# Where a norm's factor is applied in a hybrid Mamba/attention layer: on the gates by their activation, on dt, x, B and C by the eviction

## The chip, the cores and the metric

The kernel runs on one core of one Trainium2 chip. Its time is the device time of one execution in microseconds (us); the span is the part of it that the profiler's records cover. PE is the tensor engine, PEld its weight loads, DVE the vector engine, ACT the scalar engine, POOL the GpSimd engine, SP the engine that issues most of the loads.

## The reference

One layer over 512 tokens with 2048 channels, all in float32. Only the head of it matters here:

```python
h = rmsnorm(x, norm_w)          # x * rsqrt(mean(x*x) + EPS) * norm_w, one factor for each token
u = h @ w_in
z_ssm, xbc, dt_f, dt_b, q_a, kv_a, z_attn, g_ssm, g_attn = split(u)
xbc = silu(dwconv(xbc, conv_w, conv_b))      # depthwise over tokens, 4 taps
dt  = softplus(dt + dt_bias)                 # both directions
...                                          # bidirectional SSD on x, B, C, dt; silu(z_ssm) gates it
...                                          # latent attention on q_a, kv_a; silu(z_attn) gates it
y   = (ssd @ w_ps) * sigmoid(g_ssm) + (attn @ w_pa) * sigmoid(g_attn)
out = rmsnorm(x + y @ w_out)
```

The norm multiplies each token by one factor R = rsqrt(mean(x*x) + EPS). A product with h is the product with x * norm_w, with each token's result multiplied by R.

## The kernel before

Float32 products are made of three matmuls of a rounded type: each operand is split into a high part (ACT, `h` or `wh`) and a low part (DVE or POOL, `l` or `wl`), and `mm3` (L168 to L170) adds high*high, high*low and low*high in one PSUM bank. One product here means 16 such steps over the 2048 channels, 48 matmuls of 128x512, for 128 output columns and all 512 tokens. Its weights come as two chunks of 128x1024 (`wchunk`, L158 to L165): a load on SP's queue, a cast on ACT, a subtraction on DVE (on POOL while `ahead[0]` is 0, at the very start). There are three buffers of each.

The program in the order of time:

- **Head.** `cst` and `vec` come on ACT's queue. x is loaded row by row (tokens on partitions) in eight pieces (L208). For each of four token tiles ACT squares and sums the two halves (L210), DVE and ACT make the factor (L212 to L213, `small_rsqrt` L183 to L192), and L220 (DVE) or L218 (ACT) multiplies x by it in place. PE then turns x over by 64 transposes (L225) through all eight PSUM banks; ACT writes h's high part with norm_w multiplied in (L229), DVE its low part (L230), both out of PSUM.
- **First products.** First the product for dt (`dtp`), then six products of group 0 (x tiles, B and C: `xbc_gen`), each followed by the four taps of the convolution (`conv_silu`, L388 to L392: ACT with a bias, three DVE steps, ACT's Silu) and a store. Beside these products `h_sums` (L710 to L730) builds h = h_h + h_l again and from it the operand sums S1, S2, S3 and S4, and `dt_make` (L282 to L300) makes the softplus of dt in some 18 DVE steps.
- **Gates.** Three gate weights `wz`, `wgs` and `wga` of 2048x2048. Each takes two column pairs, and each pair is a Strassen-Winograd scheme of seven products (P1, P5, P6, P2, P3, P7, P4) with operands x11, x12, x22 (quadrants of h), S1, S2, S4 (held) and S3, which is loaded back from DRAM into the place of quadrant x21 at the start of `wz`; x21 is loaded and split again at the end of `wga` (`h_back`). Each result of 128x512 (tokens on partitions) passes `gate`, an activation (Silu or Sigmoid) and a store.
- **The rest.** Four groups of SSD with the other products as filling, attention, two projections, the merge, the output projection and the last norm.

The order of PE's instructions is the order of the code. A scheduler places the instructions of the other engines by priority; `tc.high_priority(offset=AHEAD)` puts the weights' chunks ahead, and `keep_in_program_order` fixes single instructions. Pools of SBUF buffers set when a buffer comes free.

## Time and profile before

| what | value |
|---|---|
| time, median of 3 runs | 2065.09 us (2063.13 to 2066.34) |
| the profiled execution's own time | 2063.24 us |
| its span | 2061.4 us |
| PE busy | 1968.5 us, 95% of the span |
| DVE busy | 1461.8 us, 71% |
| ACT busy | 967.9 us, 47% |
| POOL busy | 317.4 us, 15% |
| first matmul of a product (`dtp`) | 32.82 us after the span's start |

The page cuts the span into 40 slices of 51.5 us, with the busy share of each engine in tenths. A timeline row gives start, duration, engine, line, operation, output and inputs, shape and count, and in brackets the idle time before it with what ended it. A group row gives count, busy time and the mean ns of one. A row of windows gives, for a stretch of time, the busy time of PE, PEld, DVE, ACT and POOL with their counts, then the granted clock of PE, the share of the DMA engines and GB/s.

### The profile page before, as it was taken

The page shows a single profiled execution, that of the slowest core. Times are in us where ns is not written, and L with a number is a line of the kernel's source. Part 1 is how long each engine was busy: PE and PEld are TensorE (multiplying, and loading weights), DVE is VectorE, ACT ScalarE, POOL GpSimd, SP SyncE. Part 2 cuts the span into 40 slices and gives each one's busy share as a digit, 9 for nine tenths or more (in the row PEclk, how much of TensorE's full clock was granted, in tenths as well). Part 3 has the DMA queues.
Part 4 walks back from the last instruction along what each step waited for, and adds up shares of the span by engine and source line. Part 5 has one row for each costly group of instructions (what it writes and reads, how often), then busy time and mean ns, then how long its engine had stood idle before and what let it go on. Part 6 is the DMA issues. An engine that isn't in the chain of part 4 may idle for free.

```text
span 2061.4 us, 24706 instructions
## 1 busy us (share of the span) xinstructions
PE 1968.5 (95%) x9074; PEld 1627.2 (79%) x9074; DVE 1461.8 (71%) x1946; ACT 967.9 (47%) x1351; POOL 317.4 (15%) x337
## 2 busy tenths in 40 slices
PE   6999999999989999998999999999999999999998
PEld 5888888888868787786788878888877777888886
DVE  7976676676669789698687567666676888776342
ACT  6444444444445656445546344444444454443232
POOL 0001010010043152241331101110010201100120
PEclk9999999999999999998999999999999999999999
DMA  5568657656547847686464857783376876865332
GB/s 195 165 179 200 175 124 192 192 116 182 140 162 189 250 124 205 207 226 201 154 183 153 236 156 200 206 219 90 86 210 249 301 248 264 273 217 169 107 118 82
DMA packets 166585, 378.56 MB, mean 184 GB/s; under 512 B 16001, under 2 KB 65281, under 8 KB 165889
## 3 DMA queue, kind: packets, MB, share of 16 engines
q1 hardware_dynamic: 104688, 238.33, 35.4%
q0 software_dynamic: 26944, 92.29, 20.5%
q10 hardware_dynamic: 34832, 46.38, 6.2%
q8 instruction: 71, 1.16, 0.2%
q14 instruction: 50, 0.40, 0.1%
HBM read 325.03 MB, written 98.04 MB: 205 GB/s over the span
## 4 chain that ended last, share of the span: by engine, by line
PE 71%; DVE 13%; DMA 9%; issue 4%; ACT 3%; SPq 1%; POOL 0%; ACTq 0%; DVEq 0%; POOLq 0%
PE P L564 10%; PE P L565 10%; PE P L563 10%; PE f L1492 3%; PE f L1493 3%; PE f L1491 3%; PE za L168 2%; PE za L169 2%; DVE sum L999 2%; PE za L170 2%; PE xbc L168 2%; PE xbc L169 2%; PE xbc L170 2%; DVE wl L164 2%; DMA wraw<-wps 1%
## 5 line engine op out<-in xcount | busy, mean ns | idle before, releaser
L434 DVE TENSOR_TENSOR wl<-X,wh 128x1024 fp32r<-128x1024 f32 x152 | 185.3, 1223 | 84.5 <-ACT wh L433 83.9
L433 ACT CAST wh<-X 128x1024 fp32r<-128x1024 f32 x152 | 159.5, 1053 | 157.7 <-PE P L565 137.7
L164 DVE TENSOR_TENSOR wl<-wraw,wh 128x1024 fp32r<-128x1024 f32 (+2 forms) x148 | 172.7, 1167 | 85.7 <-ACT wh L163 85.3
L163 ACT CAST wh<-wraw 128x1024 fp32r<-128x1024 f32 (+2 forms) x150 | 145.1, 969 | 138.9 <-PE za L169 41.2
L434 DVE TENSOR_TENSOR wl<-wraw,wh 128x1024 fp32r<-128x1024 f32 x74 | 91.5, 1236 | 96.4 <-ACT wh L433 96.2
L168 PE MATMUL xbc<-h_h,wh 128*128 128x512 f32 x384 | 152.6, 397 | 0.0
L170 PE MATMUL xbc<-h_h,wl 128*128 128x512 f32 x384 | 150.5, 392 | 0.0
L169 PE MATMUL xbc<-h_l,wh 128*128 128x512 f32 x384 | 150.3, 391 | 0.0
L434 DVE TENSOR_TENSOR wl<-Y,wh 128x1024 fp32r<-128x1024 f32 x80 | 97.9, 1224 | 72.9 <-ACT wh L433 72.8
L564 PE MATMUL P<-wl,h_h 128*128 128x512 f32 x384 | 149.5, 389 | 0.0
L565 PE MATMUL P<-wh,h_l 128*128 128x512 f32 x384 | 149.5, 389 | 0.0
L563 PE MATMUL P<-wh,h_h 128*128 128x512 f32 x384 | 149.5, 389 | 0.0
L433 ACT CAST wh<-wraw 128x1024 fp32r<-128x1024 f32 x74 | 77.9, 1053 | 144.4 <-PE f L1493 69.3
L433 ACT CAST wh<-Y 128x1024 fp32r<-128x1024 f32 x80 | 84.2, 1054 | 111.7 <-PE P L565 96.8
L564 PE MATMUL P<-wl,S 128*128 128x512 f32 x288 | 112.4, 390 | 0.6 <-DVE wl L434 0.6
L565 PE MATMUL P<-wh,S 128*128 128x512 f32 x288 | 112.1, 389 | 0.0
L563 PE MATMUL P<-wh,S 128*128 128x512 f32 x288 | 112.1, 389 | 0.0
L168 PE MATMUL za<-h_h,wh 128*128 128x512 f32 x256 | 102.0, 398 | 0.0
L170 PE MATMUL za<-h_h,wl 128*128 128x512 f32 x256 | 100.5, 392 | 0.1
L169 PE MATMUL za<-h_l,wh 128*128 128x512 f32 x256 | 100.2, 391 | 0.0
L999 DVE TENSOR_TENSOR_SCAN sum<-da,scn 128x512 f32<-128x512 f32 x64 | 86.7, 1368 | 0.0
L170 PEld LDWEIGHTS xbc<-h_h,wl 128*128 128x128 f32 x384 | 72.6, 189 | 15.5
(634 smaller groups left out, 5187.8 us busy)
## 6 DMA issues: line engine op xcount, KB each, us to landing
wraw<-wi SPq DMA_DIRECT2D x102, 512.0 KB, 4.1
da<-da_d SPq DMA_DIRECT2D x64, 256.0 KB, 4.6
T_wps<-wps POOLq DMA_DIRECT2D x32, 512.0 KB, 6.2
T_wpa<-wpa POOLq DMA_DIRECT2D x32, 512.0 KB, 9.4
wraw<-wo SPq DMA_DIRECT2D x32, 512.0 KB, 3.5
wraw<-wps SPq DMA_DIRECT2D x24, 512.0 KB, 5.2
xbc_d<-xbc ACTq DMA_DIRECT2D x24, 256.0 KB, 3.5
wraw<-wun SPq DMA_DIRECT2D x16, 384.0 KB, 3.1
```

What stands on the lines that cost most here:

```text
L163: act.copy(h, raw)
L164: (dve if ahead[0] else pool).tensor_sub(l, raw, h.bitcast(F32))
L168: pe.matmul(out, wh, xh, start=start, stop=False)
L169: pe.matmul(out, wh, xl, start=False, stop=False)
L170: pe.matmul(out, wl, xh, start=False, stop=stop)
L433: act.copy(hi_, raw)
L434: dve.tensor_sub(lo_, raw, hi_.bitcast(F32))
L563: pe.matmul(bs[i], xh, wh, start=(j == 0), stop=False)
L564: pe.matmul(bs[i], xh, wl, start=False, stop=False)
L565: pe.matmul(bs[i], xl, wh, start=False, stop=(j == 7))
L999: dve.tensor_tensor_scan(sums[dd], flat(da), mask, 0.0, ALU.add, ALU.mult)
L1491: pe.matmul(acc, mh, wh, start=(start and k == 0), stop=False)
```

## The change

The host gives x a second time, transposed (`xt`: eight pieces of 128 channels x 2 x 512 tokens). The kernel loads these in place of x, interleaved with the chunks of the first three products' weights. There are no transposes any more. h_h and h_l now hold x * norm_w without the factor R, and are made from SBUF as each piece lands (L236 on ACT, L237 on DVE). ACT squares each piece (L240), POOL adds up the eight squares (`sq_sum`, L242, seven additions of 128x1024), eight small matmuls sum them over the partitions (`square_sums`, L251), and four matmuls with a diagonal spread the factor over the partitions (`factor`, L264), which ACT copies to R and stores (`r_d`). The first three products (tiles 4, 5 and 0 of group 0) go side by side in three banks in a fixed order of their steps; tiles 1, 2, 3 and then dt follow one after the other.

The factor is applied in four places: `xbc_done` multiplies the bank by R on DVE (L752) ahead of the convolution, where before the convolution read the bank itself; `dt_make` multiplies dt by R, and moves from the first products to the second pair of `wz`, with its input and R loaded back from DRAM; `gate` gives the activation R as its scale (`r4`, one number for each token on a partition); and at the last pair of `wga` hooks load all four quadrants of x * norm_w from DRAM, multiply them by R (x11 and x12 on POOL, x21 and x22 on DVE, L828) and split them anew into h_h and h_l, so that the products behind the gates find h there as before. For this x_t is multiplied by norm_w in place (16 DVE steps, L765) and stored as four quadrants (8 stores on ACT's queue, L214). `h_sums` takes its sums from x_t and has no additions of h_h and h_l any more.

Matmuls of 128x512 ahead of the gates are the same in number (eight products) but for 3 short warming ones, 8 of square_sums and 4 of factor; 64 transposes are gone.

The diff, cut to its core:

```diff
-    xs_t = []
-    for t in range(TT):
...
-    tps = [mm(), mm(), mm(), pa(), pa(), pb(), pb(), pc()]
...
+    def sxq(name):
+        n_q[0] ^= 1
+        return sx.tile([P, 1024], F32, tag=f"q{n_q[0]}", bufs=1, name=name)
+    n_q = [1]
+    def put(dst, t):
+        act.dma_start(dst, t)
+    R, v_x, sq_sum = (sx.tile([P, n], F32, name=nm) for n, nm in ((SEQ, "R"), (SEQ, "v_x"), (1024, "sq_sum")))
+    warm_ps = pc("warm")
+    dve.memset(v_x, 1.0)
+    for _ in range(3):
+        pe.matmul(warm_ps, v_x[:, 0:P], v_x, start=True, stop=True)
+    ahead[0] = 1
+    firsts_i = (T_XBC + 4, T_XBC + 5, T_XBC)
+    early = [[] for _ in firsts_i]
+    for j in range(8):
+        for n, at in ((0, 0), (1, 2), (2, 4), (0, 4), (1, 6)):
+            if at == j:
+                early[n].append(wchunk(a["wi"][firsts_i[n], len(early[n])], 1024))
+        xs = x_t[:, 2 * j:2 * j + 2, :].rearrange("p k t -> p (k t)")
+        nc.sync.dma_start(xs, a["xt"][j])
+        for k in (2 * j, 2 * j + 1):
+            nw = vec[:, V_NORM + k:V_NORM + k + 1]
+            act.activation(h_h[:, k, :], x_t[:, k, :], AF.Copy, scale=nw)
+            dve.scalar_tensor_tensor(h_l[:, k, :], x_t[:, k, :], nw, h_h[:, k, :].bitcast(F32), ALU.mult, ALU.subtract)
+        for i in ([j - 1] if 0 < j < 7 else [6, 7] if j else []):
+            sq = sxq("sq") if i else sq_sum
+            act.activation(sq, x_t[:, 2 * i:2 * i + 2, :].rearrange("p k t -> p (k t)"), AF.Square)
+            if i:
+                pool.tensor_add(sq_sum, sq_sum, sq)
+    early[2].append(wchunk(a["wi"][firsts_i[2], 1], 1024))
+    r4 = few(4)
...
+    def square_sums():
+        ss = pa("ss")
+        for t in range(TT):
+            for k in range(2):
+                pe.matmul(ss[:, t:t + 1], sq_sum[:, k * SEQ + t * P:k * SEQ + (t + 1) * P], ones[:, 0:1],
+                          start=(k == 0), stop=(k == 1))
+        v4, rt = few(4), few(4)
+        dve.tensor_scalar(v4, ss[:, 0:4], 1.0 / D, EPS, ALU.mult, ALU.add)
+        new = {"rt": rt, "rr": r4}
+        small_rsqrt(v4, 4, lambda n: new[n])
+        for t in range(TT):
+            dve.tensor_scalar_mul(v_x[:, t * P:(t + 1) * P], ident, r4[:, t:t + 1])
+    def factor():
+        rp = pc("rp")
+        for t in range(TT):
+            pe.matmul(rp[:, t * P:(t + 1) * P], ones, v_x[:, t * P:(t + 1) * P], start=True, stop=True)
+        act.copy(R, rp)
+        put(r_d, R)
...
+    dt_t = []
+    def dt_make():
+        v, e = st("dv_"), st("e")[0:64, :]
+        u, pl = (sum_tile("p1") for _ in range(2))
+        nc.sync.dma_start(v, dv_d)
+        nc.sync.dma_start(u, r_d)
+        dve.tensor_mul(v, v, u)
+        put(kr_d, v[64:128, :])
+        v, u, pl = (t[0:64, :] for t in (v, u, pl))
+        da64 = u
+        act.activation(v, v, AF.Identity, bias=vec[0:64, V_DTB:V_DTB + 1])
...
-        def whole(name, i, j):
-            t = sxq(name)
-            h, l = part_of(i, j, q)
-            dve.tensor_add(view4(t), h.bitcast(F32), l.bitcast(F32))
-            return t
         ks = slice(4 * q, 4 * q + 4)
         cs = slice(q * 1024, (q + 1) * 1024)
+        def x(i, j):
+            return x_t[:, 8 * j + 4 * q:8 * j + 4 * q + 4, i * 256:(i + 1) * 256]
         def keep(w, t):
             split_into(s_op[w][:, 0, ks], s_op[w][:, 1, ks], view4(t))
...
+        s1, s3 = sxq("s1"), sxq("s3")
+        tc.keep_in_program_order(dve.tensor_sub(view4(s1), x(1, 0), x(1, 1)))
+        keep("S1", s1)
+        tc.keep_in_program_order(dve.tensor_sub(view4(s3), x(0, 0), x(1, 0)))
         put(h_d["S3"][:, cs], s3)
-        dve.tensor_sub(x11, x22, x11)
-        keep("S2", x11)
-        x12 = whole("x12", 0, 1)
-        dve.tensor_add(x12, x12, x11)
-        keep("S4", x12)
-    for i in range(5):
-        run(xbc_gen(0, (4, 5, 0, 1, 2, 3)[i], sxt))
-        if i in (1, 3):
-            h_sums(i // 2)
-    dt_make(sxd)
+        s2 = sq_sum
+        dve.tensor_sub(view4(s2), view4(s1), x(0, 0))
+        keep("S2", s2)
+        dve.tensor_add(view4(s1), view4(s2), x(0, 1))
+        keep("S4", s1)
...
+    def xbc_done(i, p_):
+        dve.tensor_mul(v_x, p_, R)
+        o = st("xbc")
+        put(xbc_d[0][i], conv_silu(v_x, (0, 1, 2, 3, 16, 20)[i], o, lambda n: o))
+    firsts = [mm("xbc") for _ in range(3)]
+    order = "AAAABBBB" + "AABB" * 2 + "C" * 8 + "A" * 8 + "B" * 8 + "C" * 8
+    for i in together([gemm_steps(p_, win(t), h_h, h_l, w_) for p_, t, w_ in zip(firsts, firsts_i, early)], order):
+        if i == 31:
+            square_sums()
+        if i == 42:
+            factor()
+    ahead[0] = AHEAD
+    for k in range(KT):
+        tc.keep_in_program_order(dve.tensor_scalar_mul(x_t[:, k, :], x_t[:, k, :], vec[:, V_NORM + k:V_NORM + k + 1]))
+    for q in range(2):
+        for n, (j, i) in (("x11", (0, 0)), ("x12", (1, 0)), ("x21", (0, 1)), ("x22", (1, 1))):
+            put(view4(h_d[n][:, q * 1024:(q + 1) * 1024]), x_t[:, 8 * j + 4 * q:8 * j + 4 * q + 4, i * 256:(i + 1) * 256])
+    for i, p_ in zip((4, 5, 0), firsts):
+        xbc_done(i, p_)
+    for i in (1, 2, 3):
+        p_ = mm("xbc")
+        if i < 3:
+            h_sums(i - 1)
+        run(gemm_steps(p_, win(T_XBC + i), h_h, h_l))
+        xbc_done(i, p_)
+    dtp = mm("dtp")
...
+            act.activation(o, o, f, scale=r4[:, t:t + 1])
             put(dst[t][b], o)
         return done
...
+    r_back = []
+    def r_load():
+        r_back.append(st("R"))
+        nc.sync.dma_start(r_back[0], r_d)
+    def h_load(which, tag="w", in_order=False):
+        def f():
+            h_ops.raws[which] = []
+            for q in range(2):
+                t = w_tile(tag)
+                made = nc.sync.dma_start(t, h_d[which][:, q * 1024:(q + 1) * 1024])
+                if in_order:
+                    tc.keep_in_program_order(made)
+                h_ops.raws[which].append(t)
+        return f
+    def h_scale(which, i, eng):
+        def f():
+            for t in h_ops.raws[which]:
+                eng.tensor_mul(view4(t), view4(t), r_back[0][:, i * 256:(i + 1) * 256].unsqueeze(1).broadcast_to([P, 4, 256]))
+        return f
+    def h_new(which, i, j):
+        return lambda: [h_part(which, i, j, q) for q in range(2)]
...
+    gates[0].hooks = {(0, "P5"): [h_load("S3", in_order=True), h_new("S3", 1, 0)], (1, "P5"): [dt_make]}
+    gates[2].hooks = {(1, "P1"): [r_load, h_load("x11"), h_scale("x11", 0, pool), h_new("x11", 0, 0)],
+                      (1, "P2"): [h_load("x12"), h_scale("x12", 0, pool), h_new("x12", 0, 1)],
+                      (1, "P3"): [h_load("x21"), h_scale("x21", 1, dve)],
+                      (1, "P7"): [h_new("x21", 1, 0), h_load("x22", "Y"), h_scale("x22", 1, dve)],
+                      (1, "P4"): [h_new("x22", 1, 1)]}
     gates[0].first_columns(0)
-    run(xbc_gen(0, 3, None))
-    for p_ in gates:
+    first_pair = gates[0].pair(0)
+    for _ in range(24):
+        next(first_pair)
+    dv_ = st("dv_")
+    act.copy(dv_, dtp)
+    put(dv_d, dv_)
+    run(first_pair)
+    run(gates[0].pair(1))
...
```

Three places show how instructions now stand on an engine.

**Head, DVE.** Before, x was scaled (L220) and the sixteen low parts of h (L230) came out of PSUM banks in one row, the last ones of it interleaved with two chunks of weights:

```order
L220 TENSOR_SCALAR xt3_290<-xt3_290,small_65 128x1024
L230 SCALAR_TENSOR_TENSOR h_l_233<-mm_307,vec_226,h_h_232 128x512
L230 SCALAR_TENSOR_TENSOR h_l_233<-mm_308,vec_226,h_h_232 128x512
L230 SCALAR_TENSOR_TENSOR h_l_233<-mm_309,vec_226,h_h_232 128x512
L230 SCALAR_TENSOR_TENSOR h_l_233<-pa_310,vec_226,h_h_232 128x512
L230 SCALAR_TENSOR_TENSOR h_l_233<-pa_311,vec_226,h_h_232 128x512
```

Now, from the first instruction on (`wl` are low parts of weights, `h_l` those of h, x4 counts repeats):

```order
L221 MEMSET v_x 128x512
L891 TENSOR_SCALAR small<-vec 128x8
L164 TENSOR_TENSOR wl<-wraw,wh 128x1024
L237 SCALAR_TENSOR_TENSOR h_l<-x_t,vec,h_h 128x512 x4
L164 TENSOR_TENSOR wl<-wraw,wh 128x1024
L237 SCALAR_TENSOR_TENSOR h_l<-x_t,vec,h_h 128x512 x4
L164 TENSOR_TENSOR wl<-wraw,wh 128x1024
L237 SCALAR_TENSOR_TENSOR h_l<-x_t,vec,h_h 128x512 x2
L164 TENSOR_TENSOR wl<-wraw,wh 128x1024
L237 SCALAR_TENSOR_TENSOR h_l<-x_t,vec,h_h 128x512 x2
L164 TENSOR_TENSOR wl<-wraw,wh 128x1024
L237 SCALAR_TENSOR_TENSOR h_l<-x_t,vec,h_h 128x512 x4
```

On POOL seven additions (L242) stand where two subtractions of weights (L164) stood. The low parts are made from x_t in SBUF, with the weights between them, and POOL has seven additions beside them. The next row on DVE is the last early chunk, then the chain of the factor.

**The stores of x_t, ACT.** Around the end of the third product, now, with the semaphores that are waited for in brackets (DMAHW is a transfer):

```order
L214 DMA h_x12_199<-x_t_248 128x4x256 [waits DVE_49]
L265 COPY R_252<-rp_514 128x512 [waits PE_49]
L214 DMA h_x22_201<-x_t_248 128x4x256
L214 DMA r_d_361<-R_252 128x512 [waits Activation_49]
L214 DMA h_x11_198<-x_t_248 128x4x256 [waits DMAHW1_49]
L214 DMA h_x12_199<-x_t_248 128x4x256 [waits DMAHW2_49,DVE_49]
L163 CAST wh_630<-wraw_628 128x1024
L214 DMA h_x21_200<-x_t_248 128x4x256 [waits DMAHW3_49]
L214 DMA h_x22_201<-x_t_248 128x4x256 [waits DMAHW5_49]
L397 ACTIVATE xbc_561<-v_x_253,vec_228 128x512 [waits DVE_49]
L163 CAST wh_682<-wraw_680 128x1024 [waits PE_49]
L163 CAST wh_712<-wraw_710 128x1024 [waits PE_49]
```

None of these stores was there; the row before had `h_x21` and `h_S3` stores one at a time between casts. Casts of weights (L163) and the first step of the convolution (L397) are queued behind them.

**Last pair of wga, DVE, from P2's sums to P3's chunks.** Before:

```order
L591 TENSOR_TENSOR p5_3894<-p5_3894,u_3964 128x512
L591 TENSOR_TENSOR p5_3896<-p5_3896,u_3965 128x512
L434 TENSOR_TENSOR wl_4032<-wraw_4029,wh_4031 128x1024
L434 TENSOR_TENSOR wl_4057<-Y_3818,wh_4056 128x1024
L434 TENSOR_TENSOR wl_4074<-Y_3837,wh_4073 128x1024
L619 TENSOR_TENSOR p1_3812<-p1_3812,P2_3970 128x512
L619 TENSOR_TENSOR p1_3814<-p1_3814,P2_3971 128x512
L434 TENSOR_TENSOR wl_4091<-Y_3856,wh_4090 128x1024
```

Now:

```order
L603 TENSOR_TENSOR p5_3837<-p5_3837,u_3907 128x512
L603 TENSOR_TENSOR p5_3839<-p5_3839,u_3908 128x512
L442 TENSOR_TENSOR wl_3975<-wraw_3972,wh_3974 128x1024
L442 TENSOR_TENSOR h_l_235<-wraw_3997,h_h_234 128x4x256
L442 TENSOR_TENSOR wl_4010<-Y_3761,wh_4009 128x1024
L828 TENSOR_TENSOR wraw_4085<-wraw_4085,R_3747 128x1024
L442 TENSOR_TENSOR wl_4027<-Y_3780,wh_4026 128x1024
L634 TENSOR_TENSOR p1_3743<-p1_3743,P2_3913 128x512
L634 TENSOR_TENSOR p1_3745<-p1_3745,P2_3914 128x512
L442 TENSOR_TENSOR h_l_235<-wraw_3999,h_h_234 128x4x256
L442 TENSOR_TENSOR wl_4044<-Y_3799,wh_4043 128x1024
L828 TENSOR_TENSOR wraw_4087<-wraw_4087,R_3747 128x1024
```

Between the chunks of P2 and P3 (`wl` from `wraw` and from `Y`) there are now two splits of x11 (L442 with `h_l`) and two multiplications of x21 by R (L828); the loads, the multiplications on POOL and the casts on ACT ahead of the splits are other engines' rows.

151 lines of the change are left out of this document (51 added, 100 removed).

## Prediction

> **What bounds the kernel now.** The page's engine shares come first, then the waits of PE in the first 66 us, then the timeline of that stretch.
>
> ```profile
> PE 1968.5 (95%) x9074; PEld 1627.2 (79%) x9074; DVE 1461.8 (71%) x1946; ACT 967.9 (47%) x1351; POOL 317.4 (15%) x337
> PE   6999999999989999998999999999999999999998
> ...
> PE mm L225 <- DVE xt L220: 19.4, 4, 11.0
> ```
>
> PE is busy for 95% of the span, so what moves the end is a hole in PE's work. The largest stands in the first slice (6): PE waits 19.4 us there, in four pieces, for DVE's scaled x. Everything behind waits for that, since PE's order is fixed.
>
> ```profile
> 7.77 0.17 DVE L824 TENSOR_SCALAR small<-vec 128x8 f32<-128x8 f32 x1 [7.77 <-DMA vec<-vec]
> 11.04 0.90 PE L225 MATMUL mm<-cst,xt 128*128 128x128 f32 x3 [11.04 <-DVE xt L220]
> 18.33 1.03 ACT L163 CAST wh<-wraw 128x1024 fp32r<-128x1024 f32 x1
> 19.43 4.64 POOL L164 TENSOR_TENSOR wl<-wraw,wh 128x1024 fp32r<-128x1024 f32 x2 [18.55 <-ACT wh L163]
> 19.68 2.11 DVE L188 TENSOR_TENSOR small<-small 128x1 f32<-128x1 f32 x1
> 21.83 2.26 DVE L189 TENSOR_TENSOR small<-small 128x1 f32<-128x1 f32 x1
> 24.12 0.15 DVE L190 TENSOR_SCALAR small<-small 128x1 f32<-128x1 f32 x1
> 25.32 0.91 PE L225 MATMUL mm<-cst,xt 128*128 128x128 f32 x3 [6.31 <-DVE xt L220]
> 25.83 1.84 ACT L229 ACTIVATE h_h<-mm,vec 128x512 fp32r<-128x512 f32 x3
> 31.83 2.06 DVE L230 SCALAR_TENSOR_TENSOR h_l<-mm,vec,h_h 128x512 fp32r<-128x512 f32 x3
> 32.82 0.47 PE L168 MATMUL dtp<-h_h,wh 128*128 128x512 f32 x1
> 36.44 1.22 DVE L164 TENSOR_TENSOR wl<-wraw,wh 128x1024 fp32r<-128x1024 f32 x1
> 43.83 0.39 PE L168 MATMUL xbc<-h_h,wh 128*128 128x512 f32 x1
> ```
>
> From 32.82 on PE runs without a hole: one product takes 43.83 - 32.82 = 11.0 us, so a step of three matmuls takes 0.69 us. Note 19.68: two DVE operations on 128x1, which take 0.16 us elsewhere, end only as POOL's two subtractions do, one POOL subtraction each (4.64 / 2 = 2.32 us).
>
> ```profile
> 585.73 2.04 POOL L932 TENSOR_TENSOR xw<-xT,wst 128x512 f32<-128x512 f32 x2 [5.76 <-ACT xT L887]
> 587.73 5.93 POOL L965 TENSOR_TENSOR yo<-xT,dsk 128x512 f32<-128x512 f32 x4
> 589.69 2.06 DVE L164 TENSOR_TENSOR wl<-wraw,wh 128x1024 fp32r<-128x1024 f32 x1
> 598.19 1.21 DVE L164 TENSOR_TENSOR wl<-wraw,wh 128x1024 fp32r<-128x1024 f32 x1
> 663.88 3.27 POOL L1008 TENSOR_TENSOR G<-dtT,cbb 128x512 f32<-128x512 f32 x2 [11.95 <-DVE cbb L987]
> 664.78 1.53 DVE L999 TENSOR_TENSOR_SCAN sum<-da,scn 128x512 f32<-128x512 f32 x1
> 667.81 1.21 DVE L999 TENSOR_TENSOR_SCAN sum<-da,scn 128x512 f32<-128x512 f32 x1
> ```
>
> It shows again later: the same subtraction takes 1.21 us alone and 2.06 beside POOL. So a DVE operation with two inputs in SBUF and a POOL operation take turns here, each whole.
>
> **The change, part by part. The new head.** The measure is the end of the third product: 32.82 + 3 x 11.0 = 65.8 us before. Behind it both kernels still have five products, then the gates, in PE's work.
>
> Loads don't set it. Before, 4.2 MB of x and the first chunks came at about 420 GB/s:
>
> ```profile
> GB/s 0 163 289 372 407 339 423 412 418 421 426 418 76 0 0 199 188 311 0 0 0 0 0 11 0 30 298 350 257 126 0 96 191 371 128 259 90 259 90 109
> ```
>
> Each number covers 1.5 us. Now eight pieces and six chunks, 7.3 MB, take some 18 us at that rate and are there by about 21 us.
>
> ACT makes 16 h_h at 0.62 us (1.84 / 3), 5 casts at 1.0 and 8 squares at the 1.0 of a cast of that size, one or two squares behind the last h_h: from 7.8 us (vec gives norm_w) the last h_h is ready near 30 us.
>
> DVE makes 16 h_l at 0.69 us (2.06 / 3), 11.0 us, and 5 weight subtractions at 1.14 (1.22 less the overlap of neighbours), 5.7 us. POOL makes 7 additions at 2.32, 16.2 us. Before, h_l read one input from PSUM; now both tensors lie in SBUF, and none of the rows is of this operation beside POOL. Bounds: if h_l takes turns with POOL, the sum is 11.0 + 5.7 + 16.2 = 33 us from about 8, so 41 us; if POOL's addition costs the 2.04 / 2 = 1.02 us for 512 that L932 shows, 39 us; if h_l doesn't take turns, ACT sets it and the last addition ends near 33 us. I take 41, as the subtractions of two SBUF inputs are the nearest rows.
>
> The Trainium skill, page SBUF — State Buffer, section Who interferes with whom, says of this that DVE's second port is GpSimd's and that the lock is exclusive; the trace agrees with it at 19.68 and 589.69 us (2.06 for 1.21). By that rule the additions and h_l exclude each other; no run here shows it for this operation yet, and without the rule the forecast would rest on the subtractions alone.
>
> From the last h_l PE has one step left of the first product's second half, 8 small matmuls and 4 of 128 columns x 512 for the factor (0.4 and 0.9 us by the 128x128 rows: 0.90 / 3 each, overlapped), and 16 steps x 0.69 = 11.0: 41 + 0.7 + 0.4 + 0.9 + 11.0 = 54.0 us. **Gain at the head: 65.8 - 54.0 = 11.8 us**, 13.7 with the cheaper POOL, 20 without turns (last addition at 33, and 12.4 behind it: 45.7).
>
> **From the fourth product to the gates.** Before, DVE is full there:
>
> ```profile
> 60.00:80.00 20.00, 20.00 (x90) 16.58 (x89) 20.00 (x20) 14.15 (x16) 0.00 (x0) 1.00 0.44 150
> ...
> L710 DVE TENSOR_TENSOR x<-h_h,h_l 128x1024 f32<-128x1024 f32 x8 | 9.6, 1218 | 0.0
> L391 DVE SCALAR_TENSOR_TENSOR cacc<-xbc,vec,cacc 128x511 f32<-128x511 f32 x23 | 17.0, 738 | 0.1
> L220 DVE TENSOR_SCALAR xt<-xt,small 128x1024 f32<-128x1024 f32 x6 | 4.3, 752 | 0.1
> L292 DVE SCALAR_TENSOR_TENSOR pl<-pl,u 64x512 f32<-64x512 f32 x8 | 5.4, 679 | 0.1
> ```
>
> PE has 20.00 of 20 us, though, as this work began in the first product. Removed: 8 additions of L710 (9.6 us) and the 18 or so steps of dt_make at 0.68 (12 us). Added: 16 scalings by norm_w at about 0.42 (half of 752 ns and a fixed part), 6.7 us; 6 multiplications by R at 0.68, 4 us. Nothing of the operand sums can begin ahead of the scalings. These and the chain of the factor (7 small operations, about 3.5 us) lie beside the 11.8 us that PE needs from square_sums to the fourth product, almost to the end. Behind it: 14 steps of h_sums and 7 weight subtractions, 21 x 1.14 = 24 us, and 24 operations of 512 at 0.66, 16 us: 40 us of DVE in the four remaining products' 43.7 us, before DVE can split the gates' first four chunks. It doesn't wait only for itself: ACT's casts stand behind its stores, and each tap chain goes ACT, DVE three times, ACT. If its gaps add up to 9 us, PE waits about 4 to 5 us; if there are none, 0; a fully serial ACT and DVE would cost 9. **I take a loss of 3.5 us**, nearer to the filled row above, which had no hole on PE.
>
> **Gates.** The scale of the 48 activations lies on ACT, which has room:
>
> ```profile
> 480.00:500.00 20.00, 20.00 (x90) 16.58 (x89) 13.01 (x15) 9.89 (x12) 3.46 (x4) 1.00 0.86 214
> 500.00:520.00 20.00, 20.00 (x90) 16.56 (x89) 16.47 (x15) 10.17 (x12) 0.00 (x0) 1.00 0.16 30
> 520.00:540.00 20.00, 20.00 (x90) 16.55 (x89) 14.07 (x15) 8.44 (x9) 2.59 (x3) 1.00 0.64 167
> 540.00:560.00 20.00, 20.00 (x90) 16.58 (x89) 13.39 (x15) 11.84 (x14) 0.86 (x1) 1.00 0.56 150
> sum 80.00, PE 80.00 PEld 66.27 DVE 56.93 ACT 40.34 POOL 6.91; mean PE 20.00 PEld 16.57 DVE 14.23 ACT 10.08 POOL 1.73
> L187 DVE RECIPROCAL rr<-rt 128x512 f32<-128x512 f32 x2 | 6.7, 3352 | 2.1 <-ACT rt L185 2.0
> ```
>
> In the last pair, 480 to 560 us, DVE is idle for 80 - 56.9 = 23 us, ACT for 40. Added there on DVE: 6 splits and 4 multiplications at 1.22, 12.2 us; on POOL 4 multiplications of 2.32, 9.3 us, which shut DVE out by turns. Together 21.5 of the 23 us, so mean load allows it. But the first split of x11 stands on DVE between P2's and P3's chunks and waits there for SP's load and POOL's multiplication; P3's chunks are queued behind it, and PE waits for these. Bounds: 0, and 9.3 if all of POOL's time lands on PE; I take 1.7. In wz's second pair dt_make brings 18 steps of 0.68 and a reciprocal of 3.35, 15 us, into gaps of about 5.8 of 20 us: 0 to 2, I take 0.5. The 12 extra DMAs of 512 KB on SP and ACT (4 MB in, 4 MB out) meet a DMA share of 0.16 to 0.86; they cost nothing unless the landing that the split above waits for comes late, which is in its bounds. Behind the gates all order is as before.
>
> **Sum:** 11.8 - 3.5 - 1.7 - 0.5 = 6.1 us less than the profiled 2063.24, 2057.1. Its median of runs stands 1.85 above that execution, so **2059 us**.
>
> **The rivals.** (A) *h_l doesn't take turns with POOL.* For it: SCAN at 664.78, with both inputs in SBUF, takes 1.53 beside POOL and not 3; it isn't a plain tensor operation either. Against it: 1.53 isn't 1.21. Head gain 20 in place of 11.8: 2059 - 8.2 = 2051 us.
>
> (B) *DVE becomes the bound from the fourth product to the gates' end and takes the gain back.* For it: DVE's 20.00 of 20 us above, and sums that start 20 us later than before. Against it: 10 us less DVE work in all. Loss at its bounds, 9 + 2 instead of 3.5 + 2.2, gives 2059 + 5.3 = 2064 us.
>
> (C) *ACT's queue is held by the stores.* The eight stores of x_t and that of R stand in order on ACT's queue, and four of them wait for an earlier transfer to land before ACT may go on to casts. What landings cost:
>
> ```profile
> h_x<-x ACTq DMA_DIRECT2D x2, 512.0 KB, 3.1
> h_S<-s ACTq DMA_DIRECT2D x1, 512.0 KB, 5.6
> ```
>
> One chunk of the fourth product is cast ahead of them, 5.5 us of cover. Four waits of 3.1 hold ACT for 12.4 us and PE for 6.9; four of 5.6 for 22.4 and 16.9. It then stands in place of the 3.5: 11.8 - 16.9 - 2.2 = 7.3 us of loss, 2072 us. It decides from a landing of (11.8 - 2.2 + 5.5) / 4 = 3.8 us each. Against it: the stores of the first half can start while DVE scales the second, so some waits are over by then.
>
> **How the numbers follow.** Runs of this kernel differ by 3.2 us, so 0.2% (4.1 us: below 2061.0 or above 2069.2) is what can be told from no change. Forecast 0.50, of which 0.42 falls below 2061.0 and 0.08 above; A 0.15, all faster; B 0.20, 0.17 the same and 0.03 slower; C 0.15, 0.10 slower and 0.05 the same. Faster 0.57, same 0.30, slower 0.13. The range reaches from 2048 (A with the cheaper addition) to 2067 (B and half of C).
>
> **What would show it.** PE's first product starts near 10 us, and its step 33 near 42 (forecast) or 34 (A). An h_l beside a POOL addition lasts 2 us or more, or 0.75. The fourth product starts near 54. Waits of PE for L164 or L442 between 54 and 105 add up to 3 or 4 us; with C the casts L163 stand behind L214, with stores that land later than 3.8 us. In the last pair of wga the only new wait is P3's first chunk. Wrong would be a hole at a place that has none here: in PE between 20 and 40 us for a load, or behind the gates.

## Result: slower by 1.1%, and the profile after

| | median of runs | profiled execution | span |
|---|---|---|---|
| before | 2065.72 us (2063.13 to 2067.85, 4 runs) | 2063.24 us | 2061.4 us |
| changed | 2092.19 us (2081.42 to 2094.03, 4 runs) | 2091.57 us | 2089.7 us |

The ratio is 1.0113, with a 95% interval of 1.0084 to 1.0141. The medians alone give 1.0128. The forecast was 2059 us, with a range from 2048 to 2067. The page after, its first rows:

```profile
PE 1982.2 (95%) x9040; PEld 1627.2 (78%) x9040; DVE 1490.4 (71%) x1950; ACT 975.8 (47%) x1345; POOL 342.6 (16%) x346
...
PE   8999989999989999998999989999989999999998
```

The hole at the start is smaller (8 where it was 6), and a new one stands in the sixth slice (261 to 313 us, the place of dt_make; two more in the 24th and the 30th, where both kernels have the same instructions). PE's waits over the whole span:

```profile
PE P L575 <- DVE wl L442: 18.0, 16, 3.8
PE P L574 <- ACT wh L442: 16.3, 5, 4.3
...
PE xbc L169 <- DVE h_l L237: 6.7, 5, 1.8
PE dtp L170 <- DVE wl L164: 4.5, 1, 4.5
```

Before, the first two (then L564 and L563) were 5.4 and 6.7 us, and the dt product never waited. Ahead of the gates stand seven products, six of group 0 and dt (one sentence on the change counts eight, and the prediction once five behind the third where there are four; its sum used four). PE's order behind them is the same in both kernels, so the start of the same matmul can be compared in the two traces. The lag of the changed kernel, after less before:

| place on PE | lag, us | change of the lag |
|---|---|---|
| fourth product starts (57.7, was 65.6) | -7.9 | -7.9 |
| P1 of wz starts (111.5, was 109.1) | +2.4 | +10.3 |
| P5 of wz | +4.9 | +2.5 |
| from wz's second pair into wgs's first | +21.2 | +16.3 |
| just ahead of wga's second pair | +21.4 | +0.2 |
| end of its P7 | +29.7 | +8.3 |
| behind the holes that follow the gates in both (614.9, was 587.8) | +27.0 | -2.7 |
| end | +28.2 | +1.2 |

Two words for what follows. A hole is the time from the start of one matmul on PE to the start of the next, less the usual 0.23 us; the waits above give some 0.2 us less for the same hole. Half clock is a stretch in which the trace grants PE half of its clock; in the head a matmul then starts every 0.43 us, not every 0.23.

**Head.** The timeline of the changed kernel, DVE, POOL and PE:

```profile
30.10 9.09 DVE L237 SCALAR_TENSOR_TENSOR h_l<-x_t,vec,h_h 128x512 fp32r<-128x512 f32 x4
39.11 1.21 DVE L164 TENSOR_TENSOR wl<-wraw,wh 128x1024 fp32r<-128x1024 f32 x1
...
29.06 8.92 POOL L242 TENSOR_TENSOR sq_sum<-sq_sum,sq 128x1024 f32<-128x1024 f32 x3 [0.56 <-ACT sq L240]
...
35.81 0.50 PE L169 MATMUL xbc<-h_l,wh 128*128 128x512 f32 x1 [1.80 <-DVE h_l L237]
...
38.58 0.80 PE L169 MATMUL xbc<-h_l,wh 128*128 128x512 f32 x1 [1.80 <-DVE h_l L237]
...
40.88 3.41 PE L251 MATMUL ss<-cst,sq_sum 128*128 128x1 f32 x16
```

Four h_l take 9.1 us beside three additions of POOL, 2.3 us each where one takes 0.7 alone: they take turns, and the last ends at 39.1 us. PE waits for the low parts twice for 1.8 us, and then its matmuls take 0.63 us, not 0.39. The windows show why (PEclk is the third number from the end):

```profile
37.00:48.00 11.00, 9.42 (x31) 8.17 (x32) 6.82 (x16) 1.25 (x2) 0.97 (x1) 0.53 0.26 79
48.00:54.00 6.00, 6.00 (x31) 5.02 (x30) 5.76 (x15) 0.00 (x0) 0.00 (x0) 1.00 0.72 260
54.00:79.00 25.00, 25.00 (x114) 20.75 (x113) 13.56 (x16) 10.52 (x12) 0.00 (x0) 1.00 0.67 229
79.00:103.00 24.00, 19.53 (x82) 15.82 (x81) 23.96 (x26) 10.95 (x12) 0.00 (x0) 0.91 0.24 89
96.00:101.00 5.00, 0.53 (x3) 0.13 (x1) 5.00 (x6) 1.04 (x1) 0.00 (x0) 0.78 0.37 123
101.00:106.00 5.00, 5.00 (x13) 3.91 (x14) 3.63 (x5) 1.44 (x2) 0.00 (x0) 0.53 0.82 272
```

PE's granted clock is about half behind the holes: in 37 to 48 us, and again in 101 to 106 us, just after the dt product waited 4.5 us for DVE. DVE has gaps from 54 to 79 us (13.6 of 25 busy) and none from 79 to 103 (23.96 of 24). In the whole span the trace has 91.7 us of half clock, before 65.9; the last 6.4 and 7.9 us of these lie behind PE's last matmul and cost nothing, the others cost about half their length while PE has work. The place tells more than the total. From 31.5 us, where the records of the clock begin in the trace before, to the end of the gates, the changed kernel does 31.0 us of PE's work at half clock, the one before none. Behind the gates it is 36.4 us, before 44.0.

**Ahead of P1, ACT:**

```profile
108.41 0.59 ACT L847 COPY dv__1021<-dtp 128x512 f32<-128x512 f32 x1 [3.01 <-PE dtp L170]
...
109.39 0.63 ACT L401 ACTIVATE xbc<-xbc 128x512 f32<-128x512 f32 x1 [0.40 <-ACT dv__1021 L847]
...
110.42 2.94 ACT L442 CAST wh<-X 128x1024 fp32r<-128x1024 f32 x3 [0.40 <-ACT xbc L401]
```

The casts of P1's first weights stand behind the copy of the dt product, which waits for that product's end, and behind the last convolution's Silu. PE stands still from the end of the dt product, 108.4 us, to 111.5 us: a hole of 3.3 us. Another of 1.0 us and 3.4 us of half clock follow behind P1's first matmul.

**dt_make, in wz's second pair:** first SP's wait, then DVE.

```profile
SPq L284 <- DMA zs_d<-p: 11.2, 1, 11.2
...
249.94 0.69 DVE L285 TENSOR_TENSOR dv__1618<-dv__1618,p 128x512 f32<-128x512 f32 x1 [6.95 <-DMA p<-r_d]
...
255.33 3.35 DVE L295 RECIPROCAL p<-p 64x512 f32<-64x512 f32 x1
...
280.99 0.69 DVE L608 TENSOR_TENSOR p<-p,P 128x512 f32<-128x512 f32 x1 [3.94 <-DMA da_d<-p]
```

Its two buffers are p1 buffers, of which there are two. The load of R (L284) waits 11.2 us on SP until a gate's result has been stored out of one; DVE then waits 7.0 us for that load, with weights behind it. Later P3's sum (L608) waits 3.9 us for the store of dt_make's own result. PE has holes of 3.0, 0.8, 1.2, 1.2, 4.5 and 1.0 us there, and half clock at 252 and 293 us.

**Last pair of wga.** Ahead of P3, POOL and DVE:

```profile
549.20 2.87 POOL L828 TENSOR_TENSOR wraw<-wraw,R 128x1024 f32<-128x1024 f32 x1 [30.09 <-DMA wraw<-h_x]
549.73 3.42 DVE L442 TENSOR_TENSOR wl<-wraw,wh 128x1024 fp32r<-128x1024 f32 x1
553.19 3.31 DVE L442 TENSOR_TENSOR h_l<-wraw,h_h 128x1024 fp32r<-128x1024 f32 x1
```

Beside POOL's two multiplications a chunk and a split take 3.4 and 3.3 us on DVE, where a chunk without POOL takes 1.2: they take turns again, and P3 waits with a hole of 1.2 us. Then P7:

```profile
573.88 0.69 DVE L608 TENSOR_TENSOR p<-p,P 128x512 f32<-128x512 f32 x1 [2.05 <-DMA ga_d<-p]
576.21 1.22 DVE L828 TENSOR_TENSOR Y<-Y,R 128x1024 f32<-128x1024 f32 x1 [1.65 <-DMA Y<-h_x]
577.36 1.22 DVE L442 TENSOR_TENSOR wl<-Y,wh 128x1024 fp32r<-128x1024 f32 x1
```

DVE waits for the store of P2's results, then for x22's load, with P7's weights behind both: one hole of 4.1 us and 6.8 us of half clock.

### The profile page after: what moved, and what is told of

It reads as the page before. It is cut to its first block, busy times and chain, and to the rows that moved or that the text cites. A ratio compares the mean times of both kernels' runs of the same rounds, so it can differ in the third digit from the quotient of the medians.

```text
span 2089.7 us, 24703 instructions
## 1 busy us (share of the span) xinstructions
PE 1982.2 (95%) x9040; PEld 1627.2 (78%) x9040; DVE 1490.4 (71%) x1950; ACT 975.8 (47%) x1345; POOL 342.6 (16%) x346
## 4 chain that ended last, share of the span: by engine, by line
PE 65%; DVE 15%; DMA 10%; issue 5%; ACT 4%; POOL 0%; ACTq 0%; SPq 0%; DVEq 0%; POOLq 0%
PE P L575 8%; PE P L576 8%; PE P L574 8%; PE f L1563 3%; PE f L1564 3%; PE f L1562 3%; DVE wl L442 2%; PE za L168 2%; PE za L169 2%; PE za L170 2%; DVE sum L1066 2%; DVE wl L164 2%; PE xbc L169 2%; PE xbc L168 2%; PE xbc L170 2%
## 5 line engine op out<-in xcount | busy, mean ns | idle before, releaser
L442 DVE TENSOR_TENSOR wl<-X,wh 128x1024 fp32r<-128x1024 f32 x152 | 184.9, 1222 | 83.8 <-ACT wh L442 83.1
L164 DVE TENSOR_TENSOR wl<-wraw,wh 128x1024 fp32r<-128x1024 f32 (+2 forms) x150 | 175.6, 1171 | 90.2 <-ACT wh L163 89.7
L442 ACT CAST wh<-X 128x1024 fp32r<-128x1024 f32 x152 | 159.1, 1052 | 155.8 <-PE P L576 134.2
L163 ACT CAST wh<-wraw 128x1024 fp32r<-128x1024 f32 (+2 forms) x150 | 144.9, 967 | 129.8 <-PE za L169 40.5
L442 DVE TENSOR_TENSOR wl<-wraw,wh 128x1024 fp32r<-128x1024 f32 x74 | 95.7, 1295 | 97.4 <-ACT wh L442 97.2
L442 ACT CAST wh<-wraw 128x1024 fp32r<-128x1024 f32 x74 | 78.0, 1053 | 148.1 <-PE f L1564 71.6
L442 DVE TENSOR_TENSOR wl<-Y,wh 128x1024 fp32r<-128x1024 f32 x80 | 99.9, 1250 | 57.7 <-ACT wh L442 57.7
L442 ACT CAST wh<-Y 128x1024 fp32r<-128x1024 f32 x80 | 83.8, 1052 | 107.8 <-PE P L576 77.8
L575 PEld LDWEIGHTS P<-wl,h_h 128*128 128x128 f32 x384 | 73.4, 191 | 26.0 <-DVE wl L442 10.9
L169 PEld LDWEIGHTS xbc<-h_l,wh 128*128 128x128 f32 x384 | 73.4, 191 | 24.4 <-DVE h_l L237 9.3
```

The costliest lines, as they stand in the source:

```text
L163: act.copy(h, raw)
L164: (dve if ahead[0] else pool).tensor_sub(l, raw, h.bitcast(F32))
L169: pe.matmul(out, wh, xl, start=False, stop=False)
L442: made = act.copy(hi_, raw), dve.tensor_sub(lo_, raw, hi_.bitcast(F32))
L575: pe.matmul(bs[i], xh, wl, start=False, stop=False)
```

## Experiments

The theory after this reading: the head gains what turns of DVE and POOL leave; the rest is lost to waits that stand in an engine's queue ahead of weights (buffers, loads, one long chain), and every longer hole is paid again as half clock. Rivals were the load of DVE alone, and a clock that doesn't hang on the holes. Each ratio below is to the kernel before on the same chip. The intervals of runs 1 to 5 overlap with that of the change (1.0084 to 1.0141), so what these runs show is read at the place where they act.

**1. dt_make with buffers of its own.**

```diff
-        u, pl = (sum_tile("p1") for _ in range(2))
+        u, pl = (sum_tile("pad") for _ in range(2))
```

> The changed kernel, but dt_make takes its two buffers from a tag that nothing else uses (pad) in place of p1. Theory (buffers): the 16 us that PE loses in wz's second pair to wgs' first, 242 to 294 us, come from the two p1 buffers: the load of R waits for the store of an earlier result, the next results wait for dt_make's stores, and weights are queued behind both; then the holes of 0.5 us or more between 240 and 300 us are gone but for about 1, and the time falls by 13 to 17 us, to about 2077. Rival (load): DVE's 15 us chain with its reciprocal is too much for that pair; then the stall stays with the same 10 us of holes wherever the chain runs, and the time stays within 3 us of 2092.

Measured: 2080.01 us (2075.13 to 2084.37), ratio 1.0086 (1.0066 to 1.0105). Windows of this run:

```profile
132.00:148.00 16.00, 11.70 (x45) 8.45 (x44) 14.04 (x13) 10.73 (x14) 0.00 (x0) 0.94 0.13 45
240.00:270.00 30.00, 30.00 (x134) 24.83 (x133) 17.96 (x19) 15.20 (x17) 2.59 (x3) 1.00 0.92 255
270.00:300.00 30.00, 30.00 (x134) 24.84 (x133) 23.00 (x20) 14.97 (x17) 3.46 (x4) 1.00 0.47 92
```

The place has no hole any more, but the chain isn't there any more either: the scheduler moved it to 135 us, now that its loads waited for nothing, and there two holes of 1.6 and 2.3 us came with it. The lag rises by 5.8 us there, where that of the changed kernel rose by 16.3 in wz's second pair. So some 10 us went with the shared buffers, and the chain's own load, the rival, keeps 5.8 at its new place. Buffers and place changed together, so this run doesn't part the two fully.

**2. Additions of squares on DVE.**

```diff
-                pool.tensor_add(sq_sum, sq_sum, sq)
+                dve.tensor_add(sq_sum, sq_sum, sq)
```

> The changed kernel, but the seven additions of squares run on DVE, not on POOL. Theory (turns): h_l and POOL's additions exclude each other, so seven additions of about 1.15 us in DVE's own queue in place of seven of 2.3 to 2.9 beside it end the last h_l at 31 to 34 us, not at 39.1, the three holes of 1 to 2 us between 31 and 39 us shrink, the fourth product starts 5 to 10 us earlier; with no half clock after it the time falls by up to 10 us, to about 2083. Rival (ACT sets the head, the stretched h_l only fills up DVE's waiting): DVE takes over 8 us of work and the last h_l ends at 39 us or later; no gain.

Measured: 2082.06 us (2079.28 to 2086.11), ratio 1.0098 (1.0083 to 1.0113). DVE, and the window of the former half clock:

```profile
23.50 2.07 DVE L237 SCALAR_TENSOR_TENSOR h_l<-x_t,vec,h_h 128x512 fp32r<-128x512 f32 x3
...
30.22 1.41 DVE L237 SCALAR_TENSOR_TENSOR h_l<-x_t,vec,h_h 128x512 fp32r<-128x512 f32 x2
...
35.09 1.95 PE L251 MATMUL ss<-cst,sq_sum 128*128 128x1 f32 x16 [1.39 <-DVE sq_sum L242]
36.90 0.48 PE L168 MATMUL xbc<-h_h,wh 128*128 128x512 f32 x1
...
37.00:48.00 11.00, 11.00 (x54) 9.23 (x54) 8.93 (x27) 0.80 (x2) 0.00 (x0) 1.00 0.68 241
```

An h_l takes 0.7 us again, though DVE has seven operations more; the last one ends at 31.6 us, the holes ahead of it and the half clock are gone, and the fourth product starts at 48.8 us, 8.9 us earlier. Turns are shown for this form. A new hole of 1.6 us stands ahead of square_sums, for DVE's last addition, and brings no half clock here.

**3. The copy of the dt product behind two of P1's casts.**

```diff
-    for _ in range(24):
+    for _ in range(8):
-    act.copy(dv_, dtp)
+    tc.keep_in_program_order(act.copy(dv_, dtp))
```

> The changed kernel, but ACT's copy of the dt product stands behind the first two casts of the gates' first weights. Theory (queue): the hole of 3.3 us ahead of P1 and of 1.0 behind it come from this copy, which waits for the product's end with the casts queued behind it; the holes fall under 1 us and the time by 3 to 5 us, to about 2088. Rival (loads): X comes too late, since it is loaded into the place that the operand sums leave at 99 us; then the hole stays at 3 us and the time too.

Measured: 2087.15 us (2082.16 to 2093.82), ratio 1.0123 (1.0099 to 1.0147), no difference from the change's. The hole was 2.7 us in place of 3.3: behind the copy stood the next cause, the last convolution's Silu at 108.45 us, which waited for DVE. Neither expectation names that.

**4. x22 multiplied on POOL.**

```diff
-                      (1, "P7"): [..., h_scale("x22", 1, dve)],
+                      (1, "P7"): [..., h_scale("x22", 1, pool)],
```

> The changed kernel, but x22 is multiplied by R on POOL, not on DVE. Theory (queue): the hole of 4.1 us in P7 of the last pair stands because DVE's multiplication waits for x22's load with a weight chunk queued behind it; on POOL it doesn't, the hole goes and the half clock of 6.8 us right after it too: 4 to 7.5 us less, about 2085 to 2088. Rival (late weights): P7's chunks come late of themselves or POOL's longer operation shuts DVE out for as long; the hole stays at 3 us or more.

Measured: 2088.53 us (2084.97 to 2089.27), ratio 1.0129 (1.0112 to 1.0146), which can't be told from the change. At its place both expectations came true in part. The one hole of 4.1 us became three of 1.0, 2.3 and 1.6 us, more in sum; but the clock stayed at full speed:

```profile
566.00:580.00 14.00, 9.62 (x40) 6.85 (x39) 10.44 (x7) 8.16 (x9) 5.71 (x2) 1.00 0.46 156
```

In the changed kernel the same stretch reads 0.76:

```profile
572.00:586.00 14.00, 10.21 (x34) 7.74 (x33) 8.79 (x9) 6.27 (x7) 0.00 (x0) 0.76 0.54 174
```

**5. Operand sums earlier.**

```diff
-    for i, p_ in zip((4, 5, 0), firsts):
+    for n, (i, p_) in enumerate(zip((4, 5, 0), firsts)):
         xbc_done(i, p_)
+        if n < 2:
+            h_sums(n)
...
-        if i < 3:
-            h_sums(i - 1)
```

> The changed kernel, but the operand sums (h_sums) stand in the program behind the first and the second convolution, not behind the third and the fourth. Theory (late sums): DVE has gaps between 55 and 79 us and none between 79 and 103, where the sums, dt's weights and the last convolutions meet; both holes there, 4.6 us in the dt product and 3.3 us ahead of P1, come from that pile, not from DVE's total. With the sums earlier both fall under 1.5 us, the half clock after them goes, P1 starts at 99 to 104 us, not at 111.5, and the time falls by 7 to 13 us, to about 2080 to 2085. Rival (total): DVE has too much to do between the third product and the gates whatever the order; holes of 6 us or more come up elsewhere before P1, and P1 starts at 108 us or later.

Measured: 2084.34 us (2082.99 to 2088.89), ratio 1.0115 (1.0083 to 1.0147). P1 starts at 105.3 us, 6 us earlier. The hole in the dt product is gone (one of 1.4 us stands elsewhere), so it came from the order of DVE's work and not from its total. The hole ahead of P1 is still 3.3 us, behind the copy. With run 3 this points to two waits in a row there.

**6. PE kept busy through the dt product's hole.**

```diff
+            for _ in range(18):
+                pe.matmul(fill_ps, h_h[:, 0, 0:P], h_h[:, 0, :], start=True, stop=True)
```

> The changed kernel, but PE runs 18 matmuls without use (4.1 us, h_h by itself into a free bank) in the middle of the dt product, where it has its hole of 4.6 us for the weights' low part. The output is the same. Theory (a hole brings the half clock): with the hole filled the granted clock stays at 1.00 between 96 and 106 us, where it was 0.53 from 101 to 106; the end of the dt product comes some 1.7 us earlier against its start. Rival (the half clock comes with the load on the chip or with time, not with PE's idling): it stands there as before.

One run, with a profile: 2087.57 us. Its windows, to be read against the last two rows of the changed kernel above:

```profile
96.00:101.00 5.00, 4.60 (x21) 3.48 (x20) 5.00 (x6) 1.05 (x1) 0.00 (x0) 1.00 0.36 131
101.00:106.00 5.00, 5.00 (x22) 3.97 (x22) 3.62 (x5) 1.45 (x2) 0.00 (x0) 1.00 0.78 275
106.00:112.00 6.00, 1.73 (x4) 0.91 (x4) 3.73 (x5) 4.15 (x5) 0.14 (x1) 0.78 0.66 223
```

The clock stays at 1.00 while DVE, ACT and the loads do what they did. Now the hole ahead of P1 (4.0 us) is the first, and the half clock stands behind that. So a hole of PE's brings it. All stretches of half clock in these traces are multiples of 3.41 us long, but the last one of each, which the end cuts off. The Trainium skill, page TensorE: Matmul & The Clock Gate, section HAM oscillation — how this bites in real kernels, says that gaps of PE above some 3.4 us set the clock to half. The holes of 4.1 and 4.6 us agree with that, but shorter ones did it here too: single holes of 3.0 us (at 249 us) and of 2.4 us (run 2, at 245 us) brought 3.4 us of half clock, and in the head holes of 0.7, 2.0 and 2.0 us within 6.5 us were enough for 10.2 us of it.

**7. Four edits joined** (1, 2, 4 and 5).

> The changed kernel with four edits at once: buffers of their own for dt_make, additions of squares on DVE, x22 multiplied on POOL, operand sums earlier. If the causes are apart from one another, the gains add: 12 + 10 + 4 + 7 to 13 us less than 2092, about 2053 to 2059, the change's own sum of 2059 met or passed and the kernel before passed by 4 to 10 us. If they share one cause (the half clock after any hole, or DVE's total), the gains don't add, and it stays above 2065.

Measured: 2069.26 us (2064.18 to 2072.05, 10 runs), ratio 1.0035 (1.0021 to 1.005). P1 starts at 101.6 us. The gains didn't add up to the forecast: the hole ahead of P1 and that of dt_make at 135 us stayed, and each brought half clock.

**8. Two edits more** on top of run 7: the copy behind all four casts, and dt_make in wgs's first pair with its loads in program order and its reciprocal in halves.

```diff
-    for _ in range(24):
+    for _ in range(13):
-    act.copy(dv_, dtp)
+    tc.keep_in_program_order(act.copy(dv_, dtp))
...
-        nc.sync.dma_start(v, dv_d)
-        nc.sync.dma_start(u, r_d)
+        for t, d in ((v, dv_d), (u, r_d)):
+            tc.keep_in_program_order(nc.sync.dma_start(t, d))
...
-        dve.reciprocal(u, u)
+        for cs in (slice(0, 256), slice(256, SEQ)):
+            dve.reciprocal(u[:, cs], u[:, cs])
...
+    gates[1].hooks = {(0, "P2"): [dt_make]}
```

> The four edits joined, and two more: ACT's copy of the dt product behind all four casts of P1, and dt_make with its loads pinned in wgs's first pair and its reciprocal in two halves. Theory (two waits in a row ahead of P1: the last convolution's pile, gone with the earlier sums, then the copy): the hole of 3.3 us ahead of P1 and the one of 1.0 behind it fall under 1.5 us together and the half clock of 6.8 us after them goes, 6 us less; the 2.3 us hole of dt_make and its half clock of 3.4 us go, 4 us less: about 2059 to 2062 against 2069 for the four, not slower than the kernel before. Rival (something else ends P1's wait, such as the loads of X): P1's hole stays at 3 us, and the time at 2065 or more.

Measured: 2065.37 us (2061.61 to 2071.64, 12 runs), ratio 1.002 (1.0007 to 1.0033). dt_make now leaves no loss (the lag is the same from 149 to 430 us). P1's hole stays at 3.1 us, as the rival has it, but not for loads:

```profile
91.49 0.63 ACT L402 ACTIVATE xbc<-xbc 128x512 f32<-128x512 f32 x1 [2.45 <-DVE xbc L401]
...
95.85 0.63 ACT L402 ACTIVATE xbc<-xbc 128x512 f32<-128x512 f32 x1 [2.45 <-DVE xbc L401]
...
96.93 2.94 ACT L443 CAST wh<-X 128x1024 fp32r<-128x1024 f32 x3 [0.45 <-ACT xbc L402]
```

One convolution ends 4.36 us behind the other, and the casts are queued behind the last. The reading is that they follow one another because each uses the one buffer v_x; run 11 tries it.

**9. x11 and x12 multiplied on DVE too**, on top of run 8.

```diff
-    [r_load, h_load("x11"), h_scale("x11", 0, pool), h_new("x11", 0, 0)]
+    [r_load, h_load("x11"), h_scale("x11", 0, dve), h_new("x11", 0, 0)]
-    [h_load("x12"), h_scale("x12", 0, pool), h_new("x12", 0, 1)]
+    [h_load("x12"), h_scale("x12", 0, dve), h_new("x12", 0, 1)]
```

> As the run with six edits, but x11 and x12 are multiplied on DVE too, so that POOL has only x22. Theory (POOL's queue): in the last pair POOL's own loads of weights into Y stand behind its multiplications, which wait for the quadrants' loads, and come late for P7; without them P7's three holes of 1 to 2 us and P3's of 1.2 us go, 3 to 5 us less than that run. Rival (DVE full): four more operations of 1.2 us on DVE bring the same holes or larger ones; no difference or slower by up to 4 us.

Measured: 2060.42 us (2055.5 to 2066.56, 12 runs), ratio 0.9996 (0.9985 to 1.0008). P3's hole of 1.2 us went; P7's three became one of 4.3 us: P3's sums waited for the stores of P2's results out of p1. The timeline of DVE, and the landings of these stores (tile ga_d, 515 to 560 us):

```profile
540.65 0.69 DVE L609 TENSOR_TENSOR p<-p,P 128x512 f32<-128x512 f32 x1 [1.19 <-DMA ga_d<-p]
545.13 0.69 DVE L609 TENSOR_TENSOR p<-p,P 128x512 f32<-128x512 f32 x1 [3.79 <-DMA ga_d<-p]
...
DMA to landing us min/median/max: 2.0/2.0/14.0
```

P3's hole was not one of POOL's queue, as the theory had it. In run 8 POOL and DVE read:

```profile
523.83 2.96 POOL L829 TENSOR_TENSOR wraw<-wraw,R 128x1024 f32<-128x1024 f32 x1 [1.00 <-DMA wraw<-h_x]
...
524.44 3.42 DVE L443 TENSOR_TENSOR h_l<-wraw,h_h 128x1024 fp32r<-128x1024 f32 x1
```

and in run 9 the same split on DVE, with no work of POOL beside it:

```profile
525.81 1.22 DVE L443 TENSOR_TENSOR h_l<-wraw,h_h 128x1024 fp32r<-128x1024 f32 x1
```

POOL's first load into Y came behind its multiplications in run 8, but it had waited 2.5 us for DVE by then. So run 9 agrees with neither as it was put: turns of DVE and POOL explain P3, a buffer P7.

**10. P3's results of wga in other buffers**, on top of run 9.

```diff
-                o = sum_tile(self.spare if headed else "p1")
+                o = sum_tile(self.spare if headed else "pad" if w == "wga" else "p1")
```

> As the run before it (all four quadrants' products moved off POOL but x22's), and P3's two results of wga are written into buffers that nothing else uses there (pad) in place of p1. Theory (buffers again): the hole of 4.3 us in the last pair's P7 comes from DVE's sum of P3, which waits 1.2 and 3.8 us for the store of P2's results out of p1 (landing up to 14.0 us, as eight quadrant loads and POOL's loads share the DMA engines), with two weight chunks queued behind it; without that wait the hole falls under 2 us and its half clock of 6.8 us goes: 4 to 7 us less than 2060, ratio to the kernel before 0.996 to 0.998. Rival (late weights): Y's weights land late themselves (9.1 us where it was 6.6), so PE waits as long for ACT's cast; hole of 3 us or more, time within 2 us of 2060.

Measured: 2060.42 us (2055.47 to 2066.91, 12 runs), ratio 0.9989 (0.9976 to 1.0002). The hole became two of 1.1 and 1.6 us without half clock, and the lag over that pair fell from +2.4 to -0.5 us; the time can't tell it.

**11. Two buffers for the products times R**, on top of run 10.

```diff
-        dve.tensor_mul(v_x, p_, R)
+        v = sxq("v")[:, :SEQ] if 0 < i < 4 else v_x
+        dve.tensor_mul(v, p_, R)
```

> As that run, and the products times R of tiles 1, 2 and 3 go to two buffers in turn, not all to v_x. Theory (one buffer): with one v_x each convolution is a chain of 4.4 us (DVE, ACT, three times DVE, ACT) that can't overlap with the next, three of them stand one behind another between 83 and 96 us, and P1's casts are queued on ACT behind the last; with two buffers they overlap, the last Silu comes by 93 us, the hole of 3.1 us ahead of P1 and the half clock of 6.8 us fall: 4 to 7 us less again. Rival (ACT's order): the casts wait for the last convolution's Silu in any case, which can't be before its product ends and 4.4 us behind it; the hole gets shorter by less than 1 us.

Measured: 2055.47 us (2049.46 to 2069.53, 12 runs), ratio 0.997 (0.9951 to 0.9989): faster than the kernel before, and 1.4% below the change as it was. The last Silu comes at 93.0 us, and PE goes from the dt product into P1 with a hole of 0.4 us only; one of 1.0 us stands behind P1's first matmul. The windows up to P1 and behind its start:

```profile
54.00:95.00 41.00, 39.70 (x173) 31.76 (x171) 37.24 (x42) 20.71 (x24) 0.00 (x0) 1.00 0.39 135
95.00:102.00 7.00, 6.02 (x24) 4.38 (x25) 4.22 (x4) 3.76 (x5) 2.76 (x3) 1.00 0.99 346
```

P1 starts at 95.2 us, 13.9 us earlier than in the kernel before, and the clock stays at full speed. The profiled execution of this run took 2062.59 us, 7 above its median; in it P7 of wga has a hole of 2.9 us again, with 3.4 us of half clock.

**All runs by place**, the change of the lag in us in the profiled executions (as in the first table; up to 1.1 us between wgs's first pair and wga's second are left out):

| run | to P1 of wz | P1 of wz to wgs's first pair | wga's second pair and behind it | the rest |
|---|---|---|---|---|
| changed | +2.4 | +18.8 | +5.6 | +1.2 |
| 1 dt_make's buffers | +1.6 | +8.4 | +6.1 | +2.4 |
| 2 additions on DVE | -6.4 | +15.3 | +5.9 | +0.9 |
| 3 copy | +1.5 | +18.0 | +5.6 | -4.0 |
| 4 x22 on POOL | +1.6 | +13.0 | +1.9 | +4.7 |
| 5 sums earlier | -3.8 | +17.1 | +5.1 | +1.1 |
| 6 hole filled | +0.9 | +16.5 | +5.0 | +0.9 |
| 7 four joined | -7.5 | +8.7 | +1.3 | +5.9 |
| 8 six joined | -11.1 | +3.7 | +3.0 | +8.1 |
| 9 and x11, x12 on DVE | -11.2 | +4.1 | +2.5 | +1.3 |
| 10 and P3's buffers | -10.7 | +3.5 | -0.5 | +3.5 |
| 11 all | -13.9 | +4.8 | +2.0 | +6.4 |

The rest has the same instructions in all of them, and yet moves by -4 to +8 us: behind the gates PE's idle time adds up to 59 to 67 us and its work at half clock to 33 to 48 us, in one execution or the other. Runs 2 to 6 leave dt_make as it was, and the second column still goes from 13.0 to 18.0. So edits of 3 to 6 us can show at the place where they act and not in the time, and even there the rows have to show the cause.

## Why the prediction was wrong

Forecast and measured lag are 34.3 us apart (-6.1 and +28.2). Of these 3.9 stand in step 1, 6.8 in step 2, 15.8 in step 3 and 3.9 in step 4 with the holes behind the gates; 2.5 in wz's P1 and 1.4 in the rest had no step.

**Step 1, the head, gain 11.8: measured 7.9.** The step "41 us" for the last h_l held (39.1), with turns as its reason, and run 2 shows it; rival A is out. The time from there to the fourth product was mis-sized: 18.6 us, not 13.0. The half clock that was left, 39.1 to 47.6 us, cost some 4.2 of it. square_sums is put at 0.4 us and takes 1.8 at full clock (run 2, 35.09 to 36.90), which is the other 1.4.

**Step 2, fourth product to gates, loss 3.5 (bound 9): measured 10.3.** 7.9 us are holes, 2.4 half clock. The mean load allowed it ("40 us of DVE in 43.7"), but the work lay at the end. The size is that of rival B's bound; its mechanism, DVE's total, is not what run 5 shows, where the same work in another order left no hole in the dt product. What the step lacked is the order of DVE's work, ACT's queue (the copy, the Silu, then the casts) and the one buffer v_x that makes each convolution a chain of 4.4 us; with two buffers the hole ahead of P1 went (run 11). Rival C's landing was at its border, the last number here in us:

```profile
h_x<-x_t ACTq DMA_DIRECT2D x8, 512.0 KB, 3.8
```

but PE had no hole between 48 and 96 us. What the stores add to the pile behind it was not tried apart and stays open.

**Step 3, dt_make, 0.5 (0 to 2): measured 16.3 in its pair and the next.** This is the step that failed most. It counted DVE's time "into gaps" and asked nothing of the buffers: two of them are shared with results that wait for stores, so the chain waits for a store and the next results wait for the chain. The waits stand in the trace (11.2, 7.0 and 3.9 us). With buffers of its own the chain cost 5.8 us at another place (run 1), and none in wgs's first pair with its loads in order and its reciprocal in halves (run 8). So most of the loss goes with the buffers; no run gave the chain other buffers and kept it in place, and how much that alone would bring stays open.

**Step 4, the last pair, 1.7 (0 to 9.3): measured 8.3, and 5.6 with what the stretch behind it gave back.** This is in the range, for the most part at another place. The forecast had P3's first chunk, by turns of DVE and POOL, and that is right: it lost 1.2 us, and run 9 without POOL's multiplications loses none there. P7 lost 4.1 and then half clock, for a load that DVE waited for, and for the landing of a store.

**What no step had** is the price of a hole beyond its own length. Between 31.5 us and the end of the gates 31.0 us of PE's work ran at half clock, before none. That costs about 15 us, half of the 29.7 by which PE is late at the gates' end. The profile before shows half clock only as PEclk 8 in one slice of 40, far behind the gates, and the sum was made from it as if the clock were free.

With most of the holes mended the change is faster than the kernel before (run 11, ratio 0.997), by some 6 us: about what the forecast said of it as it was. That agreement is luck: the head gains 16.2 us in that run, not 11.8, and waits and half clock behind it take much of it back.

## What to carry to other kernels

When a chain of work is moved, list what its buffers and loads wait for and what is queued behind it on each in-order engine; idle time on the engine doesn't say that there is room. Where the tensor engine is the bound, cost a hole of some 3 us or more, or a few shorter ones close together, at more than its length: in these traces 3 to 10 us of half clock came with it, and half of that was lost. Read a change of several parts by the lag of the same matmul in both traces: the total here hid a gain of 8 us at the head under losses elsewhere.
